# Opening loads of a GELU MLP kernel: slices of 256 KB on two queues in place of 512 KB on one

## The chip, the cores and the metric

The kernel runs on one core of a Trainium2 chip. Its engines work side by side and meet at semaphores: TensorE (PE in the profile, its weight loads PEld), VectorE (DVE), ScalarE (ACT), GpSimd (POOL) and SyncE (SP, which here only issues DMA requests). The core has 16 DMA engines; requests reach them through queues, of which SyncE, ScalarE and GpSimd each have their own. The metric is the device time of one execution in microseconds.

## The reference

```python
m, k, n, p = 1024, 1024, 2048, 1024     # a: m x k, b: k x n, c: n x p, all fp32
h = np.matmul(a, b)
h = 0.5 * h * (1 + np.tanh(np.sqrt(2 / np.pi) * (h + 0.044715 * h ** 3)))
return np.matmul(h, c).astype(np.float32)
```

Two matrix products with a GELU (tanh form) between them.

## The kernel before

All products run on 128 x 128 tiles and accumulate in PSUM, which has eight banks of 128 x 512 fp32. The first product needs a with its contraction index on the partitions, so every 128 x 128 tile of a is turned on TensorE (a transpose against an identity matrix) and copied by VectorE from PSUM into the tile aT, which is bf16. In aT the first index is the half of the rows of a (h = 0 or 1, 512 rows each) and the second is the contraction slice k, eight slices of 128. b lies in b1 (columns 0 to 1023) and b2 (columns 1024 to 2047), c in c_sb, all bf16. The result of the first product is kept, after GELU, in hT.

The first 512 columns of b are multiplied in the plain way: tile t of 128 columns, half h, accumulates over the eight slices (functions mm1 and block). The remaining columns of b, and the whole second product, go through a scheme with seven products in place of eight (class Seven); it needs sums and differences of quarters, which VectorE and ScalarE make. All of that comes after the change and is not touched by it.

The order of work on every engine is the order in which it is written; nothing is reordered. Loads come on two queues:

- SyncE's queue brings fp32 data as it is: into sta a quarter of the contraction (256 columns of a, two slices) for one half of the rows, 512 KB at a time, and into stb slices of b. In order: a(half 0, quarter 0), b slices 0 and 1, a(1,0), a(0,1), b slice 2 (lines 75 to 79). These have to be cast to bf16 by VectorE or ScalarE (cast_a, cast_b, copy; lines 108 and 110).
- GpSimd's queue casts while it loads, into abq (a) and b1 (b). It starts behind a copy of one element of sta, the "gate" of line 81, so it starts when the first load has landed. Its order: a(1,1), b slice 3, then for quarters 2 and 3 a(0,q), b(q), a(1,q), then the rest of b and all of c. At most eight of its requests are under way: the ninth waits for the landing of the first.

PE begins with "stir" products on zeros (line 125), which compute nothing that is kept. Then it turns a(0,0), multiplies slice 0 and 1 of half 0, and so on, with the turning of the next quarter always between blocks of products. Line 145 is a transpose, line 146 VectorE's copy to aT, line 114 a product of the plain part. Line 86 loads a in GpSimd's queue, lines 89, 92, 98 and 101 load b, line 104 c.

Of the kernel before, what the change touches and what calls it, by code (L numbers as in the profile page):

```python
# [9 lines left out]
F32 = mybir.dt.float32  # L10
F32R = mybir.dt.float32r
BF16 = mybir.dt.bfloat16
# [7 lines left out]
def kernel(ctx, tc, a, b, c, out):  # L20
    nc = tc.nc
    M, K = a.shape
    _, N = b.shape
    _, P = c.shape
    H = 512
# [3 lines left out]
    av = a.rearrange("(mt p) k -> p mt k", p=128)  # L29
    bv = b.rearrange("(kt p) n -> p kt n", p=128)  # L30
# [9 lines left out]
    def slot(tag, shape, dt, name):  # L40
        return big.tile(shape, dt, name=name, tag=tag)

    def bank(i, shape=(128, H), dt=F32, name="ps"):
        return pp.tile(list(shape), dt, name=name, tag=f"bank{i}", padded_shape=None)

    def pieces(tag, bufs, shape, dt, name):
        return small.tile(shape, dt, name=name, tag=tag, bufs=bufs)

    warm = nc.const_aps.tensor(0.0, [128, 256], F32)
    ident = consts.tile([128, 128], BF16, name="ident")  # L50
    make_identity(nc, ident)
    gate = consts.tile([128, 1], F32, name="gate")
# [6 lines left out]
    aT = slot("a", [128, 2, KT, H], BF16, "aT")  # L59
    b1 = slot("b1", [128, KT, 1024], BF16, "b1")  # L60
# [2 lines left out]

    KH = KT // 2
    stb = slot("x0", [128, KT, H], F32, "stb")
    sta = slot("x1", [128, 2, 2, 4, 256], F32, "sta")
    abq = slot("x3", [128, 4, 2, 4, 256], BF16, "abq")

    def a_part(h, q):
        return av[:, 4 * h:4 * h + 4, ds(q * 256, 256)]  # L70

    def b_part(q):
        return bv[:, 2 * q:2 * q + 2, 0:H]

    nc.sync.dma_start(out=sta[:, 0, 0], in_=a_part(0, 0))
    nc.sync.dma_start(out=stb[:, 0:2], in_=b_part(0))
    nc.sync.dma_start(out=sta[:, 1, 0], in_=a_part(1, 0))
    nc.sync.dma_start(out=sta[:, 0, 1], in_=a_part(0, 1))
    nc.sync.dma_start(out=stb[:, 2], in_=bv[:, 2, 0:H])

    nc.gpsimd.tensor_copy(gate, sta[:, 0, 0, 3, 0:1])  # L81
    nc.scalar.activation(g, warm[:, 0:1], AF.Gelu_apprx_tanh)


    def cast_load_a(h, q):
        nc.gpsimd.dma_start(out=abq[:, q, h], in_=a_part(h, q))  # L86

    def cast_load_b(q):
        nc.gpsimd.dma_start(out=b1[:, 2 * q:2 * q + 2, 0:H], in_=b_part(q))  # L89

    cast_load_a(1, 1)
    nc.gpsimd.dma_start(out=b1[:, 3, 0:H], in_=bv[:, 3, 0:H])  # L92
    for q in range(2, 4):
# [5 lines left out]
    for n in range(2):  # L99
        for k in range(0, KT, 4):  # L100
            nc.gpsimd.dma_start(out=b2[:, k:k + 4, ts(n, H)],
                                in_=bv[:, k:k + 4, ds(1024 + n * H, H)])
# [3 lines left out]
    def copy(eng, dst, src):  # L106
        if eng is nc.scalar:
            nc.scalar.activation(dst, src, AF.Copy)
        else:
            nc.vector.tensor_copy(dst, src)  # L110

    def mm1(p, t, h, ks):
        for k in ks:
            nc.tensor.matmul(p, b1[:, k, ts(t, 128)], aT[:, h, k],  # L114
                             start=(k == 0), stop=(k == KT - 1))
# [6 lines left out]
    def stir(*widths):  # L122

        for w in widths:
            nc.tensor.matmul(ps[0, 3][:, 0:w], warm[:, 0:128], warm[:, 0:w],
                             start=True, stop=True, skip_group_check=True)

    def cast_a(h, q, *engs):

        ab = pieces("ab", 2, [128, 4, 256], BF16, "ab")  # L130
        for i, eng in enumerate(engs):
            w = 256 // len(engs)
            for j, e in enumerate(eng if isinstance(eng, tuple) else (eng,)):
                m = slice(2 * j, 2 * j + 2) if isinstance(eng, tuple) else slice(0, 4)
                copy(e, ab[:, m, ts(i, w)], sta[:, h, q][:, m, ts(i, w)])
        return ab

    def turn(h, q, i, ab):

        banks = i if isinstance(i, tuple) else (i,)  # L140
        pts = [bank(x, (128, 2, H), BF16, "pt") for x in banks]
        for n in range(2):
            pt = pts[n % len(pts)]
            for m in range(4):
                nc.tensor.transpose(pt[:, n, ts(m, 128)], ab[:, m, ts(n, 128)], ident)  # L145
            nc.vector.tensor_copy(aT[:, h, 2 * q + n], pt[:, n])  # L146
            yield

    def cast_b(k, *engs):
        c0 = 0  # L150
        for i, eng in enumerate(engs):
            w = (H - c0) if i == len(engs) - 1 else H // len(engs) // 128 * 128
            copy(eng, b1[:, k, ds(c0, w)], stb[:, k, ds(c0, w)])
            c0 += w

    def block(h, tiles, ks):
        for k in ks:
            for t in tiles:
                mm1(ps[h, t], t, h, (k,))
# [66 lines left out]
    zero = Seven(4, quarters(b1, H, 256), BB, [None] * 4, [None] * 4, 2)  # L226
    one = Seven(4, quarters(b2, 0, H), BB, [None] * 4, zero.t)

    stir(256, 256, 256, 256, 256)
    tn = turn(0, 0, 4, cast_a(0, 0, nc.vector))  # L230
    next(tn)
    stir(128)
    cast_b(0, nc.vector, nc.vector, nc.scalar)
    next(tn)
    stir(64)
    cast_b(1, nc.scalar)
    ab = cast_a(1, 0, nc.vector, nc.scalar)
    block(0, range(4), (0,))
    block(0, range(2), (1,))
    for _ in turn(1, 0, (7, 6), ab):  # L240
        pass
    block(0, range(2, 4), (1,))
    ab = cast_a(0, 1, (nc.scalar, nc.vector), nc.vector)
    cast_b(2, nc.scalar, nc.scalar)
    for t in range(3):
        ps[1, t] = bank(4 + t)
    zero.t[0], zero.t[1] = pair(2)
    block(1, range(3), (0,))
    tn = turn(0, 1, 7, ab)
    next(tn)  # L250
    block(1, range(3), (1,))
    next(tn)
# [1 line left out]
    for q in range(1, 3):  # L254
        k = 2 * q
        block(0, range(4), (k,))
        tn = turn(1, q, 7, abq[:, q, 1])
# [5 lines left out]
        tn = turn(0, q + 1, 7, abq[:, q + 1, 0])  # L263
# [10 lines left out]
    tn = turn(1, 3, 0, abq[:, 3, 1])  # L274
# [213 lines left out]
```

## Time and profile before

| | us |
|---|---|
| median of 3 runs | 117.2 (117.19 to 117.28) |
| the profiled execution's own time | 117.6 |
| its span | 115.8 |
| PE busy | 110.7 |
| VectorE, ScalarE, GpSimd busy | 90.1, 51.4, 17.3 |
| first load of a, issue to landing | 3.7 |
| granted clock of TensorE | 1.0 of full |

The span is the stretch of the program that the profiler shows, and the execution's time includes what lies around it. A busy PE is not PE at its peak, since products overlap: the mean of 379 ns of a 128 x 512 product in bf16 is longer than the distance from one to the next. In a timeline row stand the start, the length from the first start to the last end of a merged group, the engine, the line, the operation with its tiles, the count, and in brackets the idle time before it with what ended that. A row of the windows gives for each engine the busy time and the number of its instructions, then the granted clock, the mean busy share of the DMA engines (over 1 where records overlap) and the GB/s that they wrote.

### The profile page before, as it was taken

Reading aid. Unit: us, or ns where it says so; the run is one execution under the profiler, and the core shown is the slowest. Engines: PE = TensorE matmul, PEld = TensorE weight load, DVE = VectorE, ACT = ScalarE, POOL = GpSimd, SP = SyncE. Lnnn points to the kernel's source line nnn. Section 1 sums busy time; section 2 is a strip of 40 time slices with the busy share of each in tenths; the row PEclk is TensorE's granted clock in tenths of the full one; section 3 lists DMA queues with packets and bytes.
Section 4 is the critical chain, followed back from the end, with each engine's and each line's share of the span. In section 5 each row is a group of like instructions: output and inputs, shape, how many; then the busy total and the mean of one; then the engine's idle time right before and its main releaser. Section 6 shows DMA issues by size and latency. Waiting matters only on the chain.

```text
span 115.8 us, 1473 instructions
## 1 busy us (share of the span) xinstructions
PE 110.7 (96%) x544; PEld 77.1 (67%) x550; DVE 90.1 (78%) x108; ACT 51.4 (44%) x86; POOL 17.3 (15%) x29
## 2 busy tenths in 40 slices
PE   7889999999999999999999999999999999999990
PEld 6545555445777447888886444588888888888870
DVE  0247747689999998944789999999999986964581
ACT  5053000799268998066699339700043992000000
POOL 2497754222332000000000000000000000000000
PEclk9999999999999999999999999999999999999999
DMA  3999999999999999998000000070000002004994
GB/s 74 296 381 221 200 199 204 204 207 207 205 210 210 211 212 212 212 210 163 9 0 0 6 0 0 0 272 0 0 0 0 0 0 94 2 27 173 364 358 166
DMA packets 13414, 15.94 MB, mean 138 GB/s; under 512 B 736, under 2 KB 9184, under 8 KB 13408
## 3 DMA queue, kind: packets, MB, share of 16 engines
q0 software_dynamic: 8672, 9.31, 47.6%
q1 hardware_dynamic: 4592, 6.42, 15.7%
q10 hardware_dynamic: 144, 0.13, 0.3%
q8 instruction: 4, 0.07, 0.2%
q14 instruction: 2, 0.02, 0.0%
HBM read 20.97 MB, written 4.19 MB: 217 GB/s over the span
## 4 chain that ended last, share of the span: by engine, by line
PE 79%; DMA 13%; POOL 5%; issue 0%; DVE 0%
PE ps L212 76%; DMA abq<-in_a_dram 10%; DMA sta<-in_a_dram 3%; POOL abq L86 3%; PE ps L114 2%; POOL b L89 1%; POOL gate L81 1%; PE pt L145 1%; POOL b L92 0%; DVE ot L375 0%
## 5 line engine op out<-in xcount | busy, mean ns | idle before, releaser
L212 PE MATMUL ps<-x,s 128*128 128x512 f32 x128 | 29.6, 391 | 0.0
L212 PEld LDWEIGHTS ps<-x,s 128*128 128x128 f32 x128 | 24.0, 188 | 5.1
L212 PE MATMUL ps<-x,x 128*128 128x512 f32 x96 | 22.9, 394 | 0.0
L212 PEld LDWEIGHTS ps<-x,x 128*128 128x128 f32 x96 | 18.0, 188 | 3.9
L114 PE MATMUL ps<-aT,b 128*128 128x512 bf16 x62 | 15.7, 379 | 0.3 <-DVE b L110 0.2
L298 ACT ACTIVATE v<-ps 128x512 f32<-128x512 f32 x10 | 6.0, 598 | 19.1 <-PE ps L212 19.1
L212 PE MATMUL ps<-c_sb,hT 128*128 128x512 bf16 (+2 forms) x78 | 14.1, 336 | 0.1
L212 PE MATMUL ps<-x 128*128 128x512 f32 x56 | 13.2, 393 | 0.0
L212 PEld LDWEIGHTS ps<-x 128*128 128x128 f32 x56 | 10.2, 188 | 2.7 <-ACT u L298 0.4
L212 PEld LDWEIGHTS <-hT 128*128 128x128 bf16 x80 | 7.1, 98 | 7.0 <-issue 0.5
L118 ACT ACTIVATE hT<-ps 128x512 bf16<-128x512 f32 x14 | 7.3, 596 | 9.6 <-PE ps L114 9.6
L118 ACT ACTIVATE hT<-ot 128x512 bf16<-128x512 f32 x18 | 10.4, 623 | 2.1 <-DVE ot L303 2.0
L146 DVE COPY aT<-pt 128x512 bf16<-128x512 bf16 x16 | 6.7, 422 | 5.5 <-PE pt L145 5.4
L212 PE MATMUL ps<-aT,b 128*128 128x512 bf16 x46 | 10.6, 379 | 0.1
L303 DVE TENSOR_TENSOR ot<-ps,u 128x512 f32<-128x512 f32 x10 | 6.7, 688 | 5.2 <-ACT u L298 5.2
L303 DVE TENSOR_TENSOR ot<-ps,v 128x512 f32<-128x512 f32 x10 | 6.7, 688 | 4.9 <-DMA out_dram<-ot 3.9
L170 DVE TENSOR_TENSOR x<-c_sb 128x1024 fp32r<-128x1024 bf16 x8 | 9.2, 1216 | 0.0
L114 PEld LDWEIGHTS <-b 128*128 128x128 bf16 x64 | 5.7, 97 | 4.5 <-DVE b L110 0.3
L212 PEld LDWEIGHTS <-b 128*128 128x128 bf16 x48 | 4.6, 97 | 5.7 <-issue 0.3
L104 POOL DMA_DIRECT2D c_sb<-in_c_dram x8 | 5.6, 703 | 13.4 <-DMA b<-in_b_dram 11.1
L170 DVE TENSOR_TENSOR x<-b 128x1024 fp32r<-128x1024 bf16 (+1 forms) x4 | 7.0, 1751 | 0.6 <-issue 0.6
L298 ACT ACTIVATE u<-ps 128x512 f32<-128x512 f32 x10 | 5.9, 597 | 3.4 <-PE ps L212 3.2
(44 smaller groups left out, 110.7 us busy)
## 6 DMA issues: line engine op xcount, KB each, us to landing
c_sb<-in_c_dram POOLq DMA_DIRECT2D x8, 512.0 KB, 19.7
out_dram<-ot SPq DMA_DIRECT2D x14, 256.0 KB, 2.1
b<-in_b_dram POOLq DMA_DIRECT2D x6, 512.0 KB, 15.6
sta<-in_a_dram SPq DMA_DIRECT2D x3, 512.0 KB, 6.2
abq<-in_a_dram POOLq DMA_DIRECT2D x5, 256.0 KB, 8.0
stb<-in_b_dram SPq DMA_DIRECT2D x1, 512.0 KB, 5.4
b<-in_b_dram POOLq DMA_DIRECT2D x2, 256.0 KB, 8.3
stb<-in_b_dram SPq DMA_DIRECT2D x1, 256.0 KB, 7.2
```

The source lines that it names most:

```text
L81: nc.gpsimd.tensor_copy(gate, sta[:, 0, 0, 3, 0:1])
L86: nc.gpsimd.dma_start(out=abq[:, q, h], in_=a_part(h, q))
L89: nc.gpsimd.dma_start(out=b1[:, 2 * q:2 * q + 2, 0:H], in_=b_part(q))
L104: nc.gpsimd.dma_start(out=c_sb[:, t:t + 2], in_=cv[:, t:t + 2])
L114: nc.tensor.matmul(p, b1[:, k, ts(t, 128)], aT[:, h, k], start=(k == 0), stop=(k == KT - 1))
L118: nc.scalar.activation(hT[h][:, t], p, AF.Gelu_apprx_tanh)
L145: nc.tensor.transpose(pt[:, n, ts(m, 128)], ab[:, m, ts(n, 128)], ident)
L146: nc.vector.tensor_copy(aT[:, h, 2 * q + n], pt[:, n])
L170: nc.vector.tensor_tensor(out=dst[:, r], in0=x[:, r], in1=y[:, r], op=op)
L212: nc.tensor.matmul(p[:, ds(c0, w)], l[:, k, ts(j, 128)], r[:, k, ds(c0, w)], start=(start and k == 0), stop=(k == self.kt - 1), skip_group ...
L298: nc.scalar.activation(st, p, AF.Copy)
L303: nc.vector.tensor_tensor(out=ot, in0=p, in1=st, op=ADD)
```

## The change

The loads on SyncE's queue are now slices of 128 columns of a for one half of the rows, 256 KB each: a(0) and a(1) of slice 0, then of slice 1. The two b slices are issued by ScalarE, the first at once, the second behind the activation that loads its table. a(0, quarter 1) and b slice 2 go from SyncE's queue to the head of GpSimd's, as loads that cast. Each slice of a is cast and turned by itself, half by half of its four row tiles; the casts are split between VectorE and ScalarE (those of a's first slice run on VectorE alone), and b's are all on ScalarE. The last wide stir is 128 instead of 256 columns. Half 1 of slice 0 is multiplied before half 0 of slice 1. The two slices are turned in PSUM banks 6 and 7.

```diff
-    sta = slot("x1", [128, 2, 2, 4, 256], F32, "sta")
+    sta = slot("x1", [128, 8, 4, 128], F32, "sta")
...
-    nc.sync.dma_start(out=sta[:, 0, 0], in_=a_part(0, 0))
-    nc.sync.dma_start(out=stb[:, 0:2], in_=b_part(0))
-    nc.sync.dma_start(out=sta[:, 1, 0], in_=a_part(1, 0))
-    nc.sync.dma_start(out=sta[:, 0, 1], in_=a_part(0, 1))
-    nc.sync.dma_start(out=stb[:, 2], in_=bv[:, 2, 0:H])
-
-    nc.gpsimd.tensor_copy(gate, sta[:, 0, 0, 3, 0:1])
+    def load_a(h, k):
+        nc.sync.dma_start(out=sta[:, 2 * k + h], in_=av[:, 4 * h:4 * h + 4, ts(k, 128)])
+
+    def load_b(eng, k):
+        eng.dma_start(out=stb[:, k], in_=bv[:, k, 0:H])
+
+    load_a(0, 0)
+    load_b(nc.scalar, 0)
+    load_a(1, 0)
+    load_a(0, 1)
+    load_a(1, 1)
+
+    nc.gpsimd.tensor_copy(gate, sta[:, 0, 3, 0:1])
     nc.scalar.activation(g, warm[:, 0:1], AF.Gelu_apprx_tanh)
+    load_b(nc.scalar, 1)
...
+    cast_load_a(0, 1)
+    nc.gpsimd.dma_start(out=b1[:, 2, 0:H], in_=bv[:, 2, 0:H])
     cast_load_a(1, 1)
...
+    def cast_a(h, k, *parts):
+        m0 = 0
+        for eng, m in parts:
+            r = slice(m0, m0 + m)
+            copy(eng, ab[k][:, h, r], sta[:, 2 * k + h][:, r])
+            m0 += m
+
+    def turn_one(h, k):
+        for m in range(4):
+            nc.tensor.transpose(pt[k][:, h, ts(m, 128)], ab[k][:, h, m], ident)
+
+    def keep_one(h, k):
+        nc.vector.tensor_copy(aT[:, h, k], pt[k][:, h])
...
-    stir(256, 256, 256, 256, 256)
-    tn = turn(0, 0, 4, cast_a(0, 0, nc.vector))
-    next(tn)
+    ab = [pieces("ab", 2, [128, 2, 4, 128], BF16, "ab") for k in range(2)]
+    pt = [bank(6 + k, (128, 2, H), BF16, "pt") for k in range(2)]
+    stir(256, 256, 256, 256, 128)
+    cast_a(0, 0, (nc.vector, 2), (nc.vector, 2))
+    turn_one(0, 0)
+    keep_one(0, 0)
     stir(128)
-    cast_b(0, nc.vector, nc.vector, nc.scalar)
-    next(tn)
+    cast_b(0, nc.scalar, nc.scalar)
     stir(64)
-    cast_b(1, nc.scalar)
-    ab = cast_a(1, 0, nc.vector, nc.scalar)
-    block(0, range(4), (0,))
-    block(0, range(2), (1,))
-    for _ in turn(1, 0, (7, 6), ab):
-        pass
-    block(0, range(2, 4), (1,))
-    ab = cast_a(0, 1, (nc.scalar, nc.vector), nc.vector)
-    cast_b(2, nc.scalar, nc.scalar)
+    cast_a(1, 0, (nc.vector, 2), (nc.scalar, 2))
+    cast_a(0, 1, (nc.vector, 2), (nc.scalar, 2))
+    block(0, range(2), (0,))
+    turn_one(1, 0)
+    keep_one(1, 0)
+    block(0, range(2, 4), (0,))
+    turn_one(0, 1)
+    keep_one(0, 1)
+    cast_b(1, nc.scalar, nc.scalar)
+    cast_a(1, 1, (nc.vector, 2), (nc.scalar, 2))
     for t in range(3):
         ps[1, t] = bank(4 + t)
     zero.t[0], zero.t[1] = pair(2)
     block(1, range(3), (0,))
-    tn = turn(0, 1, 7, ab)
+    block(0, range(2), (1,))
+    turn_one(1, 1)
+    keep_one(1, 1)
+    block(0, range(2, 4), (1,))
+    tn = turn(0, 1, 7, abq[:, 1, 0])
     next(tn)
```

More of the change, by code (lines that the diff above doesn't have):

```diff
@@ L126, in stir @@
                              start=True, stop=True, skip_group_check=True)
[L128 to L136, printed above, removed]
+    def cast_a(h, k, *parts):
[9 more added lines that the diff above has]
+        nc.vector.tensor_copy(aT[:, h, k], pt[k][:, h])
     def turn(h, q, i, ab):
```

## The prediction

> **What bounds the kernel now.** I read the page's engine table first, then the chain that ended last, the timeline of the first 25 us, one-microsecond windows of the DMA traffic, and the waits of each engine. Throughout, X.XX is us from the span's start, and a "row" is a line of such a view.
>
> ```profile
> span 115.8 us, 1473 instructions
> PE 110.7 (96%) x544; PEld 77.1 (67%) x550; DVE 90.1 (78%) x108; ACT 51.4 (44%) x86; POOL 17.3 (15%) x29
> ...
> 0.74 3.70 DMA sta<-in_a_dram
> ...
> 10.15 11.43 DMA abq<-in_a_dram
> 21.58 0.05 issue
> 21.63 0.40 PE pt L145 x4
> ...
> 24.87 2.81 PE ps L212 x13
> ```
>
> The span is PE: from 21.63 the chain is PE with gaps of 0.05 us. So only what happens before about 22 us can be changed by new loads, and the first question is where PE falls behind there. The chain names one DMA issued at 10.15, but the timeline says more:
>
> ```profile
> 5.14 0.88 POOL L86 DMA_DIRECT2D abq<-in_a_dram  x1
> 6.90 1.47 PE L114 MATMUL ps<-aT,b 128*128 128x512 bf16 x6 [0.17 <-DVE b L110]
> 10.03 0.39 PE L145 MATMUL pt<-ident,ab 128*128 128x128 bf16 x4
> 11.63 1.48 POOL L98 DMA_DIRECT2D b<-in_b_dram  x2 [0.66 <-DMA abq<-in_a_dram]
> 13.68 0.74 POOL L101 DMA_DIRECT2D b<-in_b_dram  x1 [0.56 <-DMA abq<-in_a_dram]
> 14.99 0.74 POOL L101 DMA_DIRECT2D b<-in_b_dram  x1 [0.57 <-DMA b<-in_b_dram]
> 15.99 0.24 PEld L145 LDWEIGHTS <-abq 128*128 128x128 bf16 x4 [0.30 <-DMA abq<-in_a_dram]
> 16.02 0.39 PE L145 MATMUL pt<-ident,abq 128*128 128x128 bf16 x4
> 16.23 0.74 POOL L101 DMA_DIRECT2D b<-in_b_dram  x1 [0.50 <-DMA abq<-in_a_dram]
> 17.56 0.74 POOL L101 DMA_DIRECT2D b<-in_b_dram  x1 [0.59 <-DMA abq<-in_a_dram]
> 21.62 0.23 PEld L145 LDWEIGHTS <-abq 128*128 128x128 bf16 x4 [0.64 <-DMA abq<-in_a_dram]
> ```
>
> First real product: 6.90. From 10.03 the groups "four transposes and three or four products" follow each other every 0.9 to 1.1 us, which is their own work. PE is then gated by work and by loads almost equally: at 15.99 the weight load waits for a(half 1, quarter 2), which landed at 15.95 by its last semaphore record. The POOL rows give the rate of its queue: each request waits for the landing of the one eight places ahead, and 512 KB of fp32 land every 1.31, 1.24 and 1.33 us, mean 1.29 us (400 GB/s read).
>
> ```profile
> 3.00:4.00 1.00, 1.00 (x4) 0.78 (x3) 0.00 (x0) 0.00 (x0) 0.00 (x0) 1.00 1.07 351
> 4.00:5.00 1.00, 0.79 (x4) 0.35 (x2) 0.54 (x1) 0.00 (x0) 0.51 (x1) 1.00 0.97 262
> 5.00:6.00 1.00, 0.67 (x6) 0.50 (x7) 0.51 (x2) 0.00 (x0) 1.00 (x2) 1.00 0.94 276
> 7.00:8.00 1.00, 1.00 (x6) 0.48 (x5) 0.32 (x2) 0.56 (x3) 1.00 (x3) 1.00 1.10 387
> 14.00:15.00 1.00, 1.00 (x10) 0.57 (x9) 0.89 (x2) 0.00 (x0) 0.43 (x2) 1.00 1.44 197
> ```
>
> Last two columns: DMA share and GB/s written. All 16 engines are full from 2 us on (in the last row 197 GB/s written is twice that read, because POOL's queue casts). While the first b load runs (4 to 6) the rate falls to 262 and 276; with 1 KB rows of a it is 387. In the packet records POOL's first packet starts only at 8.82, 3.68 us after its issue, and each engine takes it up as that engine's SyncE packets end (8.89 to 9.76, mean 9.21): POOL's loads wait until SyncE's are through. I call 9.21 the hand-over.
>
> **The change, part by part.**
>
> *The DMA sum.* Up to a(1,2) the same 4.5 MB come in both kernels; 0.75 MB (a(0,1) and slice 2 of b) move from SyncE's queue to the head of POOL's. Before, a(1,2) landed 15.95 - 9.21 = 6.74 us after the hand-over; with 0.75 MB more, at 1.29 per 0.5 MB, that is 6.74 + 1.94 = 8.68. So the change is neutral if its hand-over is at 9.21 - 1.94 = 7.27. When is it? Model: first packet at 2.0; a with its packet time; b with its own. Check on before: 1.5 MB of a at 46 ns per 1 KB packet on 16 engines (356 GB/s) 4.42; the first 512 KB of b at about 270 (windows 4 to 6) 1.94; the last 256 KB at 84 ns per 2 KB (390) 0.67; sum with 2.0: 9.03, so 0.2 of start-up is missing. After: 1 MB of a now in rows of 512 B. No load of before has those; the final 64 KB stores do, at 27 ns (303 GB/s), hence 3.46; the ends are 3.46 and 2.7 (the 387 of window 7). The 512 KB of b: 1.94 as in windows 4 to 6, or 1.34 at 84 ns. I take the row nearest to each: the same 512 KB of b as the slow ones, the same 512 B packet. 2.0 + 0.2 + 3.46 + 1.94 = 7.6 (bounds 6.24 and 7.6). a(1,2) then lands at 7.6 + 8.68 = 16.28, 0.33 later than 15.95; PE had 0.07 to spare (16.02), so it is late by 0.26.
>
> *POOL.* The gate copy waits for the first a load, now 256 KB beside 256 KB of b: the same bytes as before, 4.3 against 4.44; gate 0.70, issue at 5.0 instead of 5.14. Two more issues (0.88, 0.55 as L86 and L92 now) stand before the rest; at 0.75 each against 1.29 of transfer they cost nothing while eight are in flight. The ninth request is now b's last pair and waits for a(0,1), the tenth is a(1,3): issued at about 10.5, needed in the queue at 17, hidden by 6 us. What is open is how soon after 5.0 POOL's first packet can run: at most 3.68 us (8.68, 1.4 late against 7.27), at least its 0.88 of issue (5.9, hidden behind 7.6). I take hidden, since before the engines themselves were the visible cause. The Trainium skill (DMA: Bandwidth & Descriptors, "Latency and other measured facts") gives about 1 us for the first byte from POOL; the hand-over would then hide it, and no run here shows it alone. The same page ("Queues, rings and completion order") says that an engine alternates between queue rows packet by packet; by that, POOL's loads would share from about 6.4, the last 0.4 MB of SyncE's would take twice as long and PE's start would be 0.8 late. The row differs: no POOL packet ran before an engine was through with SyncE's, and the row decides.
>
> *SyncE and ScalarE queues.* SyncE issues four instead of five, 0.42 to 0.51 each, from 0.74 to 2.7, each under 0.85 us of transfer: covered. ScalarE issues b0 at 0.74 and b1 behind table load (1.28) and activation (0.20), at about 2.7: 0.5 each in front of casts that start after 4; covered by the wait of 4.4 for stb. b1's first packet comes at 2.7 + 1.25 = 3.95, while a's are running: no hole.
>
> *PE, VectorE, ScalarE up to the group that stood at 10.03.* Landing of a00 4.3; two 128x256 casts of 0.28 (before one of 0.69); four transposes to 5.35 (0.40); copy 0.42, so 5.8. The stirs of 128 and 64 behind it (0.44, 0.39) hold PE to 6.2; one 256 stir less 0.4 ahead is idle time. b0's two ScalarE casts (0.42 each) end before 5.5. From 6.2: eleven products at 0.215 to 0.23 and three transposes at 0.25 to 0.40: 3.1 to 3.7, so 9.3 to 9.9, if casts keep up. VectorE has the cast of a01 queued ahead of the copy of a10's transpose; a01 lands around 6.7, copy to 7.6, and its first user (half 1, slice 0) stands at 7.5 to 8. ScalarE casts a10, a01, b1 (twice), a11 in that order, 0.42 each: the last lands about 8.2, so 8.65, transposes 9.05, copy 9.5, and the next group uses the same bank, about 9.6 to 9.9. This is before 10.03, so PE's earlier start (6.2 against 6.90) is worth up to 0.4 and is then given back at the wait for a(1,2).
>
> *Behind 16.* PE is filled by its own work until a(1,3), which landed at 21.58 although 15 of its 16 engines were through by 19.92: a 16 KB instruction fetch started at 19.57 on the last one. The fetch goes by PE's place in the program, so it moves with PE: 0. Later loads shift by the same 0.3; nothing past 30 us waits for one.
>
> Sum: +0.26 on the profiled execution, whose own time is 117.6 with a span of 115.8 and 1.8 around it; it stands 0.4 above the median of the three runs, 117.2. Forecast 117.2 + 0.26 = 117.5. No change is within 0.2%, 0.23 us, about what a measurement can tell.
>
> **The rivals.**
> 1. *Hand-over early, gain.* If 512 B rows and the two hardware queues together run at the 387 of window 7, and b at 390, the hand-over comes at 6.24; POOL's first packet, if it takes 1.9 (its bounds are 0.88 and 3.68), at 6.9. Then a(1,2) lands at 15.6, 0.37 early, and PE's 9.6 allows it: 116.8. A gain is decided by a hand-over before 7.0. For it: b's slow windows may have been a first touch that now overlaps a's packets. Against it: 27 ns per 512 B.
> 2. *Break-even.* Half of b slow: 2.0 + 0.2 + 3.46 + 1.64 = 7.3; PE unchanged, 117.2.
> 3. *POOL's first packet late.* 3.68 after 5.0: hand-over 8.68, a hole in DMA traffic from about 7.5; 1.4 late less 0.07: 118.5. For it: the 3.68 is the only latency shown. Against: it coincides engine by engine with the end of SyncE's packets.
> 4. *b behind a.* If ScalarE's queue waits behind SyncE's as POOL's did, b0 lands at about 6.5 and ScalarE's seven casts (2.9) end at 9.4, transposes and copy 10.3: PE 0.3 late, 117.5, the same as the forecast by another road.
>
> **How the numbers follow.** Forecast 0.30, rival 4 0.07, rival 3 0.10 (slower: 0.47), rival 2 0.24, rival 1 0.29. The range has rival 1's 0.6 gain with half of a further early hand-over below (116.6) and rival 3 above (118.5); beyond are about 1 in 10 below and 1 in 12 above. The forecast's own range is 117.4 to 117.9.
>
> **What would show it.** Right: 512 B packets near 27 ns; POOL's first packet near 7.6; the first product near 6.2; a weight load waiting for abq near 16.3; nothing new after 22. Wrong: POOL's first packet before 7.0 with PE ahead (rival 1), a fall of DMA share to near 0 about 7 to 8 (rival 3), ScalarE's b casts first at 6.5 (rival 4), or a stall of PE on VectorE's a01 cast.

## The result and the profile after

The changed kernel takes 121.25 us (121.12 to 121.37) beside 117.21 us of the kernel before on the same chip: a ratio of 1.0343, 95% interval 1.0325 to 1.0361. That is 4.0 us slower. The forecast was 117.5 us with a range up to 118.5: the sign was right, the size was not. The profiled execution took 121.37 us with a span of 119.6; against the profiled execution of before (117.6, span 115.8) both are 3.8 us longer.

From the page, the span, the engine table and the shares of the chain:

```profile
span 119.6 us, 1481 instructions
PE 112.6 (94%) x550; PEld 78.1 (65%) x550; DVE 89.5 (75%) x107; ACT 51.2 (43%) x87; POOL 18.1 (15%) x31
...
PE 84%; DMA 10%; POOL 2%; DVE 0%; issue 0%
```

The chain that ended last, cut to where it changes hands:

```profile
0.74 5.53 DMA sta<-in_a_dram
...
8.71 7.02 DMA b<-in_b_dram
...
15.78 1.04 PE ps L123 x4
...
19.73 0.40 PE pt L159 x4
...
28.27 88.03 PE ps L226 x408
```

The work of PE from the first product of the seven-product scheme on is as long as it was; it starts at 28.27 where it had started at 24.87, 3.4 us later. (The other 0.4 us of the span lie behind VectorE's last sum.) So the loss is all made before 28 us, and two loads carry it: the first one, of 256 KB, needs 5.53 us where 512 KB had needed 3.70, and slice 3 of b, the fourth request of GpSimd's queue, needs 7.02 us from its issue, most of it behind slice 2. The timeline shows what each does to PE:

```profile
6.02 0.72 ACT L117 ACTIVATE b<-stb 128x256 bf16<-128x256 f32 x2 [3.32 <-DMA stb<-in_b_dram]
6.30 0.49 DVE L119 CAST ab<-sta 128x256 bf16<-128x256 f32 x2 [6.30 <-DMA sta<-in_a_dram]
6.57 0.87 POOL L93 DMA_DIRECT2D abq<-in_a_dram  x1
6.65 0.61 PE L147 MATMUL pt<-ident,ab 128*128 128x128 bf16 x4 [1.69 <-POOL gate L87]
7.44 0.55 POOL L99 DMA_DIRECT2D b<-in_b_dram  x1
7.90 1.06 PE L123 MATMUL ps<-aT,b 128*128 128x512 bf16 x2
12.13 0.38 PE L159 MATMUL pt<-ident,abq 128*128 128x128 bf16 x4
15.78 1.04 PE L123 MATMUL ps<-aT,b 128*128 128x512 bf16 x4 [0.81 <-DMA b<-in_b_dram]
19.73 0.23 PEld L159 LDWEIGHTS <-abq 128*128 128x128 bf16 x4 [0.49 <-DMA abq<-in_a_dram]
```

The casts of a start at 6.30 (before: first a landed at 4.44), GpSimd's first request goes out at 6.57 (5.14), PE stands idle for 1.69 us and makes its first product at 7.90 (6.90), and that pair of products takes 1.06 us where six had taken 1.47: the second starts 0.43 after the first, twice the distance of 0.22 that the same products have at full clock. The clock record of after begins at 9.76, so the clock column of the windows says nothing of this moment; the distance does. The four transposes of a(0, quarter 1) follow at 12.13, where those of before stood at 10.03. Then PE waits for b at 15.78 and for a(1, quarter 2) at 19.73; the same wait stood at 15.99 before. The DMA windows show the two holes (the last two columns are the share of the DMA engines and the GB/s written):

```profile
2.00:3.00 1.00, 1.00 (x3) 0.78 (x3) 0.00 (x0) 0.69 (x2) 0.00 (x0) 1.00 0.61 162
3.00:4.00 1.00, 1.00 (x4) 0.77 (x3) 0.00 (x0) 0.00 (x0) 0.00 (x0) 1.00 0.90 144
...
10.00:11.00 1.00, 1.00 (x9) 0.52 (x7) 0.62 (x2) 0.00 (x0) 1.00 (x3) 1.00 1.15 102
11.00:12.00 1.00, 1.00 (x8) 0.51 (x7) 0.35 (x1) 0.00 (x0) 1.00 (x2) 1.00 0.77 43
12.00:13.00 1.00, 0.92 (x8) 0.51 (x7) 0.50 (x2) 0.00 (x0) 0.92 (x2) 1.00 1.02 125
13.00:14.00 1.00, 1.00 (x9) 0.51 (x7) 0.55 (x2) 0.00 (x0) 0.70 (x1) 1.00 1.42 197
```

From 3 to 4 us 144 GB/s arrive (before 351) although the engines are 0.90 busy: the packets themselves are slow. From 10 to 13 the queue of GpSimd writes 102, 43 and 125 where 197 is its normal rate. The packet records name the packets: in the first hole the 2 KB packets of slice 0 of b, at a median of 164 to 277 ns in the half microseconds from 3.0 to 4.5 and up to 651 (84 ns later); in the second hole the 1 KB packets of slice 2 of b in GpSimd's queue, up to 1333 ns (98 ns later).

The same records put the hand-over (the mean end of SyncE's packets) at 8.05. The prediction's own rule, a(1,2) lands 8.68 us after the hand-over, gives 16.73; it landed at 19.69. Hence the arithmetic that the runs below have to explain: 0.78 us from a hand-over later than the neutral 7.27, and 2.96 us behind the hand-over, where the second hole lies, together the 3.74 by which a(1,2) is late. The rule sets a mean over the 16 engines (the hand-over) against the last of them (the landing). In the changed kernel the last engine is 0.83 behind the mean when a(1,2) lands (18.86 and 19.69), in the kernel before 0.38 (15.57 and 15.95). By the means, 2.5 us are left for the hole, and 0.45 is that the engines end further apart. (In the six kernels below that have no second hole, what the rule leaves by the means is under 0.2.)

### The profile page after: what moved, and what is told of

The parts are those of the page before. It is cut to its first block, busy times and chain, and to the rows that moved or that the text cites. A ratio compares the mean times of both kernels' runs of the same rounds, so it can differ in the third digit from the quotient of the medians.

```text
span 119.6 us, 1481 instructions
## 1 busy us (share of the span) xinstructions
PE 112.6 (94%) x550; PEld 78.1 (65%) x550; DVE 89.5 (75%) x107; ACT 51.2 (43%) x87; POOL 18.1 (15%) x31
## 4 chain that ended last, share of the span: by engine, by line
PE 84%; DMA 10%; POOL 2%; DVE 0%; issue 0%
PE ps L226 74%; PE ps L123 8%; DMA b<-in_b_dram 6%; DMA sta<-in_a_dram 5%; PE pt L159 2%; POOL abq L93 1%; POOL b L99 0%; POOL gate L87 0%; DVE ot L396 0%
## 5 line engine op out<-in xcount | busy, mean ns | idle before, releaser
L123 PE MATMUL ps<-aT,b 128*128 128x512 bf16 x64 | 17.2, 392 | 0.8 <-DMA b<-in_b_dram 0.8
L226 PE MATMUL ps<-aT,b 128*128 128x512 bf16 x48 | 10.7, 379 | 0.0
L160 DVE COPY aT<-pt 128x512 bf16<-128x512 bf16 x12 | 5.1, 424 | 6.3 <-PE pt L159 6.3
```

Source lines behind the costliest of these rows:

```text
L123: nc.tensor.matmul(p, b1[:, k, ts(t, 128)], aT[:, h, k], start=(k == 0), stop=(k == KT - 1))
L226: nc.tensor.matmul(p[:, ds(c0, w)], l[:, k, ts(j, 128)], r[:, k, ds(c0, w)], start=(start and k == 0), stop=(k == self.kt - 1), skip_group ...
```

## The experiments

Four causes are on trial. *Late queue*: GpSimd's queue has the second hole because it is started late. *Two queues*: b on ScalarE's queue holds up the first load of a. *Slices*: a in rows of 512 B makes the fp32 loads longer in itself. *Clock*: PE's idle time costs it its clock. The rival to *two queues*, for the first hole, is that b's reads are slow by themselves, whoever issues them. Times are medians, ratios go against the kernel before on the same chip (117.2 to 117.4); positions within a kernel come from its profiled execution.

| kernel | us | ratio, 95% interval | first a landed | SyncE's end, mean | first b of GpSimd's queue: issue, first packet | a(1,2) landed | PE takes it up |
|---|---|---|---|---|---|---|---|
| before | 117.2 | 1 | 4.44 | 9.21 | 6.01, 10.35 | 15.95 | 16.02 |
| after | 121.25 | 1.034 (1.033 to 1.036) | 6.28 | 8.05 | 7.44, 9.81 | 19.69 | 19.73 |
| move alone | 119.24 | 1.017 (1.013 to 1.020) | 4.30 | 6.79 | 5.87, 8.35 | 17.56 | 17.61 |
| move, early queue | 117.49 | 1.001 (0.998 to 1.004) | 4.17 | 7.17 | 3.87, 8.00 | 16.19 | 16.24 |
| b on ScalarE alone | 119.93 | 1.025 (1.020 to 1.029) | 6.35 | 9.09 | 7.92, 10.31 | 17.22 | 18.54 |
| after, early queue | 120.20 | 1.023 (1.017 to 1.029) | 6.19 | 8.06 | 5.62, 8.98 | 17.11 | 18.83 |
| after, b pair in GpSimd's queue | 120.61 | 1.027 (1.020 to 1.033) | 6.18 | 7.94 | 7.36, 9.63 | 18.47 | 18.77 |
| after, more stirs | 120.65 | 1.029 (1.021 to 1.037) | 6.20 | 8.06 | 7.37, 9.52 | 18.93 | 18.98 |
| after, early queue and stirs | 119.11 | 1.014 (1.008 to 1.021) | 6.33 | 7.98 | 5.61, 8.92 | 17.32 | 17.39 |
| after, all on SyncE | 118.65 | 1.012 (1.009 to 1.015) | 3.35 | 8.08 | 4.52, 8.77 | 16.77 | 16.81 |
| the same, b as one pair behind one a | 118.88 | 1.013 (1.009 to 1.017) | 3.39 | 8.10 | 4.56, 9.08 | 17.23 | 17.27 |
| the same, b pair behind two a | 120.30 | 1.025 (1.022 to 1.029) | 3.39 | 8.03 | 4.56, 8.77 | 17.25 | 19.10 |

The last two columns say what holds PE at a(1, quarter 2): where they are within 0.1 us, PE waits for the load; where they are further apart, PE comes late by itself.

### The move to GpSimd's queue alone

The kernel before, with only a(0, quarter 1) and slice 2 of b moved to the head of GpSimd's queue; everything else, the 512 KB loads too, stays.

```diff
-    nc.sync.dma_start(out=sta[:, 0, 1], in_=a_part(0, 1))
-    nc.sync.dma_start(out=stb[:, 2], in_=bv[:, 2, 0:H])
...
+    cast_load_a(0, 1)
+    nc.gpsimd.dma_start(out=b1[:, 2, 0:H], in_=bv[:, 2, 0:H])
     cast_load_a(1, 1)
...
-    ab = cast_a(0, 1, (nc.scalar, nc.vector), nc.vector)
-    cast_b(2, nc.scalar, nc.scalar)
...
-    tn = turn(0, 1, 7, ab)
+    tn = turn(0, 1, 7, abq[:, 1, 0])
```

> The kernel before with one part of the change alone: a(0,1) and slice 2 of b move from SyncE's queue to the head of GpSimd's. The three 512 KB loads stay as they are. Theory A (moving 0.75 MB to GpSimd's queue costs nothing as long as that queue is ready when SyncE's ends): hand-over at about 7.3, no slow window, time 117.0 to 117.6. Theory B (a single slice of b at the head of GpSimd's queue is read slowly there): the window around b slice 2 falls below 130 GB/s written and the time is 119 or more.

Measured: 119.24 us (118.79 to 119.58). The hand-over came at 6.79, half a microsecond before the neutral 7.27, so by the prediction's rule this kernel should have gained; a(1,2) would have landed at 15.47. It landed at 17.56, because the hole is there in full. The windows of this kernel:

```profile
8.00:9.00 1.00, 0.92 (x11) 0.66 (x11) 0.51 (x3) 0.31 (x1) 1.00 (x2) 1.00 1.26 154
9.00:10.00 1.00, 0.94 (x6) 0.25 (x4) 0.36 (x2) 0.00 (x0) 1.00 (x3) 1.00 0.59 38
10.00:11.00 1.00, 1.00 (x10) 0.62 (x11) 0.42 (x1) 0.00 (x0) 1.00 (x2) 1.00 0.58 51
```

So the second hole needs neither the slices of 256 KB nor ScalarE's queue: the move alone brings it, and costs 2.0 us.

### The same move with an early queue

Here GpSimd does not wait for the first load of a; a fill of two tiles of c_sb, which the loads of c overwrite later, takes the place of the gate copy.

```diff
-    nc.gpsimd.tensor_copy(gate, sta[:, 0, 0, 3, 0:1])
+    nc.gpsimd.memset(c_sb[:, 12:14], 0.0)
```

> The kernel before with a(0, quarter 1) and slice 2 of b moved to the head of GpSimd's queue, as in the run that made this move alone, but GpSimd's first request does not wait for the first load of a: the gate copy is replaced by a fill of two tiles of c_sb (one such fill took 1.8 us), so the first request goes out near 3 instead of 5.0. Theory that a late start of that queue makes its first b request slow: no stretch under 150 GB/s written between 8 and 12, SyncE's packets still end near 6.8, a(1,2) lands near 15.5 (6.8 + 8.68), PE goes at its own pace: 116.6 to 117.3. Rival, that slice 2 of b is slow in that queue whenever it comes first: a stretch of 40 to 60 GB/s again within 7 to 11, a(1,2) near 17.5, 118.8 to 119.6 as with the late start. A middle case, that the early requests take bytes from the first fp32 loads: first a load after 4.8, SyncE's end after 7.3, 117.3 to 118.2.

Measured: 117.49 us beside 117.27, ratio 1.0007 (0.9979 to 1.0035): no difference from before. GpSimd's first request and the same windows:

```profile
3.00 0.87 POOL L84 DMA_DIRECT2D abq<-in_a_dram  x1
```

```profile
8.00:9.00 1.00, 1.00 (x11) 0.51 (x10) 0.43 (x1) 0.63 (x1) 0.82 (x1) 1.00 1.38 202
9.00:10.00 1.00, 1.00 (x9) 0.50 (x7) 0.76 (x2) 0.00 (x0) 0.31 (x1) 1.00 1.39 194
10.00:11.00 1.00, 1.00 (x9) 0.53 (x8) 0.42 (x1) 0.00 (x0) 1.00 (x2) 1.00 1.36 199
```

The hole is gone, and nothing but the start of GpSimd's queue was changed (3.00 in place of 5.00). The same slice of b, in the same place of the same queue, is read at full rate when its request has waited 4.1 us before its first packet, and slowly when it has waited 2.5. That settles, for this queue behind SyncE's loads, the theory of the late queue against its rival; how the late start makes the reads slow is not shown. The middle case has a small part in it: SyncE's end moved from 6.79 to 7.17 and a(1,2) came at 16.19, not 15.5, and PE took it up 0.22 later than in the kernel before, as much as the time is above 117.27. The time is 0.2 above the interval named, and not a gain.

### The changed kernel with an early queue

```diff
-    nc.gpsimd.tensor_copy(gate, sta[:, 0, 3, 0:1])
+    for t in (12, 14):
+        nc.gpsimd.memset(c_sb[:, t:t + 2], 0.0)
```

> The changed kernel with GpSimd's queue no longer behind the first load of a: two fills of a part of c_sb that is loaded later stand in place of the gate copy, so that its first request goes out at about 4 to 5 instead of 6.57. Theory D (the 16 engines run dry at the hand-over and then start GpSimd's queue together, and b's slice 2 is read slowly because of that): no slow stretch from 10 to 13, a(1,2) lands at about 17, time 118 to 118.8. Theory B: the stretch stays and the time is above 120.5. Had GpSimd's packets to share with the hardware queues, the last fp32 load would land after 10 instead of 9.20.

Measured: 120.20 us (119.00 to 120.46), 1.05 less than the changed kernel. The second hole is gone here too: 219, 192, 186 and 198 GB/s written in the windows from 8 to 12. The time is above the 118 to 118.8 that theory D named, because PE does not use the loads:

```profile
7.00:8.00 1.00, 0.85 (x7) 0.71 (x8) 0.62 (x3) 0.34 (x1) 1.00 (x2) 0.99 1.19 329
8.00:9.00 1.00, 1.00 (x6) 0.48 (x5) 0.90 (x2) 0.67 (x3) 1.00 (x3) 0.50 1.43 219
9.00:10.00 1.00, 1.00 (x6) 0.44 (x4) 0.43 (x2) 0.74 (x3) 1.00 (x2) 0.50 1.31 192
10.00:11.00 1.00, 1.00 (x7) 0.63 (x6) 0.43 (x2) 0.00 (x0) 0.69 (x2) 0.50 1.36 186
```

The third number from the end is the granted clock: 0.50 from 7.97 to 11.39 by the clock record, after a stretch of full clock from 4.56 to 7.97 in which PE had stood idle for 1.74 us. PE comes to the transposes of a(0, quarter 1) at 12.84 and is bound by its own work behind that; it takes up a(1, quarter 2) 1.7 us after its landing at 17.11:

```profile
12.84 0.38 PE L160 MATMUL pt<-ident,abq 128*128 128x128 bf16 x4
18.83 0.39 PE L160 MATMUL pt<-ident,abq 128*128 128x128 bf16 x4
```

Two stretches of 3.41 us: the Trainium skill (TensorE: Matmul & The Clock Gate, "What's actually happening") gives windows of about 3.4 us at whose end the clock is set by how busy PE was, and this record agrees.

This run also shows when GpSimd's packets run: its first request went out at 4.74, its first packet came at 7.64 on engines that SyncE's packets had left, and the last fp32 load was not delayed (9.11 against 9.20).

### Slices 2 and 3 of b as one request in GpSimd's queue

```diff
-    nc.gpsimd.dma_start(out=b1[:, 2, 0:H], in_=bv[:, 2, 0:H])
+    cast_load_b(1)
     cast_load_a(1, 1)
-    nc.gpsimd.dma_start(out=b1[:, 3, 0:H], in_=bv[:, 3, 0:H])
```

> The changed kernel with slices 2 and 3 of b in one 512 KB request of GpSimd's queue, between a(0,1) and a(1,1), as the later quarters have it. If the slow stretch from 10 to 13 belongs to requests of a single slice, it is gone: a(1,2) lands at about 17, time near 120.2 (as with the early queue, where the stretch was gone too). If it belongs to b being read by engines that start together, it stays, and may be longer: 121 or more.

Measured: 120.61 us (120.39 to 120.81), 0.6 less than the changed kernel. The hole is milder (93 GB/s written in its lowest window, where the changed kernel falls to 43), a(1,2) lands at 18.47, and PE runs at half clock from 8.35 to 11.77. So fewer and larger requests don't remove the hole. That they soften it is not shown: the kernel with more stirs below has the requests of the changed kernel, and its hole is milder too (59 GB/s written, a(1,2) at 18.93). The time fell between the two that the expectation named, and this run does not choose between causes.

### b on ScalarE's queue alone

The kernel before, with its 512 KB pair of b issued by ScalarE at 0.74.

```diff
-    nc.sync.dma_start(out=stb[:, 0:2], in_=b_part(0))
+    nc.scalar.dma_start(out=stb[:, 0:2], in_=b_part(0))
```

> The kernel before with the 512 KB load of b slices 0 and 1 issued by ScalarE instead of SyncE, nothing else. Theory C (two hardware queues that start together delay the first load of a, because b's slow packets take turns with it): the first load of a lands at 5.5 to 6.5 instead of 4.44, GpSimd's queue is issued that much later, time 117.8 to 119. Rival (queues share, bytes are bytes): the first load of a lands under 5.2 and the time is within 0.4 of 117.2.

Measured: 119.93 us (119.75 to 120.65), 2.7 slower than before, with one word changed. The timeline:

```profile
6.37 0.69 DVE L110 CAST ab<-sta 128x1024 bf16<-128x1024 f32 x1 [6.37 <-DMA sta<-in_a_dram]
7.12 0.61 PE L145 MATMUL pt<-ident,ab 128*128 128x128 bf16 x4 [1.74 <-POOL gate L81]
9.05 2.12 PE L114 MATMUL ps<-aT,b 128*128 128x512 bf16 x6
```

The first load of a lands at 6.35 in place of 4.44. The packet records say how: from 3.0 to 5.0, SyncE's queue moves 57, 47, 33 and 56 packets per half microsecond, and ScalarE's 57, 46, 32 and 53. The engines take as many packets of one queue as of the other, so each 1 KB packet of a (46 ns) has a 2 KB packet of b beside it, and those are the ones that take long. The Trainium skill (DMA: Bandwidth & Descriptors, "Queues, rings and completion order") has that alternation; between these two queues the run agrees, while GpSimd's packets, as the early queue showed, wait until an engine has nothing of SyncE's; there the measurement differs from the page, and it decides. PE stands at half clock until its clock record begins at 10.37 (its products are 0.43 apart at 9.05), and is bound by its own work afterwards: a(1,2) landed at 17.22 and was taken up at 18.54.

The second hole is here as well (169, 56 and 74 GB/s written from 10 to 13), on slice 3 of b, the first b request of GpSimd's queue in this kernel, which waited 2.4 us. So it does not hang on slice 2, and with SyncE's packets running until 9.09 it is not that the engines had run dry before it.

### All fp32 loads of the changed kernel in SyncE's queue

```diff
-    load_b(nc.scalar, 0)
+    load_b(nc.sync, 0)
     load_a(1, 0)
     load_a(0, 1)
+    load_b(nc.sync, 1)
     load_a(1, 1)
...
-    load_b(nc.scalar, 1)
```

> The changed kernel with all six fp32 loads in SyncE's queue, in the order a0 of slice 0, b slice 0, a1 of slice 0, a0 of slice 1, b slice 1, a1 of slice 1. Theory C: the first a lands at about 3.5 instead of 6.28, GpSimd issues at about 4.2 and is ready long before SyncE's queue ends; if the slow stretch from 10 to 13 comes from GpSimd's queue starting late, it goes too, and the time is 117 to 118. Theory B (slice 2 of b is slow in GpSimd's queue by itself): the stretch stays and the time is 119.5 to 120.5.

Measured: 118.65 us (118.43 to 118.89): 2.6 of the 4.0 us are back, though the time stays above the 117 to 118 of theory C. Windows and timeline of this kernel:

```profile
3.00:4.00 1.00, 1.00 (x4) 0.77 (x3) 0.49 (x2) 0.00 (x0) 0.59 (x2) 1.00 0.96 137
4.00:5.00 1.00, 1.00 (x10) 0.90 (x8) 0.00 (x0) 0.00 (x0) 1.00 (x2) 1.00 0.57 113
```

```profile
3.65 0.87 POOL L93 DMA_DIRECT2D abq<-in_a_dram  x1
6.38 0.61 PE L123 MATMUL ps<-aT,b 128*128 128x512 bf16 x2 [0.94 <-ACT b L117]
16.81 0.23 PEld L159 LDWEIGHTS <-abq 128*128 128x128 bf16 x4 [0.54 <-DMA abq<-in_a_dram]
```

The first a lands at 3.35, so the gate opens at 3.65 by itself, no second hole follows, and PE's first product (6.38) is earlier than that of before. One step undoes the first a's delay, the clock gap and the late queue at once. What is left: the hand-over is at 8.08 as in the changed kernel, 0.81 behind the neutral 7.27, and a(1,2) lands at 16.77, 0.82 behind 15.95. Here the rule of the prediction (8.08 + 8.68 = 16.76) is exact. The first hole is still there, with slice 0 of b in the same queue as a (packets up to 1036 ns): the slow first reads of b don't come from the second hardware queue. That queue only decides whether a has to wait for them.

### b as one pair in SyncE's queue, at two places

Both kernels have b's two slices as one request of 512 KB in SyncE's queue, the first behind one slice of a, the second behind two.

```diff
     load_a(0, 0)
-    load_b(nc.scalar, 0)
+    nc.sync.dma_start(out=stb[:, 0:2], in_=b_part(0))
     load_a(1, 0)
...
-    load_b(nc.scalar, 1)
```

> The changed kernel with its fp32 loads in SyncE's queue alone and b slices 0 and 1 in one 512 KB request, as before: a0 of slice 0, the b pair, a1 of slice 0, a0 and a1 of slice 1. Slicing a, the move to GpSimd's queue and the order of casts and products stay. Theory H (the loss comes from b: two queues at once and single slices of b; the slicing of a costs little): first a at 3.35, b pair at about 5.7, SyncE's packets end at 7.3 to 7.6, a(1,2) at 16.1 to 16.4, time 117.2 to 118.0, which is what the prediction's sum describes. Rival (the 512 B rows of a, or b slice 2 in GpSimd's queue, cost the rest): 118.5 or more.

> As the other of this pair, with both halves of a's slice 0 ahead of the b pair. Theory H with b slow only where it runs behind a single request of a: b's packets stay at 84 ns longer, SyncE's packets end at 7.2 or earlier, time 117.0 to 117.8; PE starts a little later (b lands at about 6.2). If b's first read is slow wherever it stands, the end of SyncE's packets is the same as in the other and the time equal or up to 0.4 longer.

Measured: 118.88 us (118.26 to 119.95) and 120.30 us (119.75 to 121.37), both above what theory H named. Their SyncE's packets end at 8.10 and 8.03, not at the 7.3 to 7.6 that a cost of splitting b would have left. So the split of b is not what makes the hand-over late. In all eight kernels here with a in 512 B rows SyncE's end lies between 7.94 and 8.10, whichever queue b is in and however it is cut; the two kernels that load the same 1.5 MB with a in 1 KB rows end at 6.79 and 7.17. 1 MB of a costs 2048 x 27 ns / 16 = 3.46 us in 512 B packets and 1024 x 46 / 16 = 2.94 in 1 KB packets, so by this estimate 0.5 of the 0.9 to 1.3 us is the price of shorter rows. The rest was not separated.

The second of the two also shows the clock again. Its pair of b landed at 7.75:

```profile
8.24 1.04 PE L122 MATMUL ps<-aT,b 128*128 128x512 bf16 x2 [2.70 <-ACT b L116]
```

PE, idle for 2.70 us, then works at half clock from 8.07 to 11.48 and comes to a(0, quarter 1) at 13.11 (11.18 in the first, which kept its clock in the profiled execution). The executions of the first price the clock directly: three were granted a mean of 0.997 to 1.0 and took 118.3 to 118.4 us, three 0.983 to 0.986 and took 119.3 to 120.0, 1.2 us more in the median. At full clock, then, the first is no slower than the kernel with six single requests in SyncE's queue (118.4 to 118.9).

### More stirs, alone and with the early queue

Four more wide products on zeros bridge PE's wait for the first a.

```diff
-    stir(256, 256, 256, 256, 128)
+    stir(256, 256, 256, 256, 256, 256, 256, 256, 128)
```

> The changed kernel with four more stirs of 256 columns at its start, so that PE does not stand idle from 4.96 to 6.65. Theory W (PE's clock fell to half in that gap, which alone costs nothing, since PE waits for loads at 15.78 and 19.73): first products 0.22 instead of 0.43 apart, time 120.8 to 121.4 as before. Rival (the slow clock is on the path): 119.5 or less.

> Both: GpSimd's queue early, as in the run before, and four more stirs. With the slow stretch of the loads gone, PE's slow clock was what held the early kernel at 120.2: its chain from 8.6 to 12.8 should shrink by 1.5 to 2 us. Theory W: 118.2 to 118.8, with PE waiting for a(1,2) at about 17.0. If the clock had no part in it: 120 again.

Measured: 120.65 us (120.55 to 121.32), 0.6 less than the changed kernel; and together with the early queue 119.11 us (118.88 to 119.45), 2.1 less, and 1.1 less than the early queue alone. The first pair of products now takes its usual time, and PE waits for a(1, quarter 2) in both kernels (below, the first two rows are of the stirs alone, the third of both):

```profile
7.58 0.59 PE L123 MATMUL ps<-aT,b 128*128 128x512 bf16 x2
18.97 0.23 PEld L159 LDWEIGHTS <-abq 128*128 128x128 bf16 x4 [0.53 <-DMA abq<-in_a_dram]
17.36 0.23 PEld L160 LDWEIGHTS <-abq 128*128 128x128 bf16 x4 [0.31 <-DMA abq<-in_a_dram]
```

Without the second hole the clock is worth 1.1 us: the early queue alone leaves PE behind its loads, and with the stirs it waits for them again. With the hole nothing is shown to hang on the clock. The changed kernel also waits for a(1,2), and the stirs' 0.6 us go with a landing 0.76 earlier (18.93 against 19.69), although stirs touch no load; the intervals of the two ratios overlap (1.021 to 1.037 and 1.033 to 1.036). That is theory W, with a time a little under the 120.8 that it named. With both causes gone the kernel is still 1.4% slower than before: PE waits for a(1,2) at 17.36, with the hand-over at 7.98 and the first a at 6.33.

### Reads by themselves

Two kernels that only read asked whether b's slow packets are a matter of the first touch or of what runs beside them.

```diff
+    read_a(0, one_a[0])
+    read_a(1, one_a[0])
+    for k in range(8):
+        read_b(nc.sync, k, one_b[0])
...
```

> Leaves out all of the computation: it only reads and writes back something. In SyncE's queue, 256 KB each and each waiting until the one before has landed: two slices of a, the eight slices of b (512 columns), the same eight again, four slices of a; then eight slices of b (the next 512 columns) back to back; then four pairs of b slices, one after the other; then in GpSimd's queue four slices of b one after the other and four back to back. Theory L (16 engines that start a slice of b at the same moment get in each other's way): every b slice that waits for the one before is slow, the second time as well, 2 us of packets or more, packets near 250 ns; the slices of a are not; back to back only the first is slow. Theory F (the first touch of b is slow): only the first slice of b, or each slice the first time, is slow; the second pass runs at 84 ns a packet, 256 KB in about 0.7 us of packets.

```diff
+    apart()
+    first()
+    load(second, bv[:, 0, 0:H])
+    apart()
...
```

> Leaves out all of the computation: nine trials of two requests in SyncE's queue, the second right behind the first, with everything landed in between. Trials: 1 and 2, a slice of a (256 KB, rows of 512 B) and then slice 0 of b (rows of 2 KB, 8 KB apart); 3, a slice of a and another; 4, a and a pair of b slices (512 KB); 5, a and the same slice of b as two requests of 256 columns; 6, slice 1 of b and then slice 0; 7, a and slice 5 of b at other columns; 8, a and 128 rows of c (2 KB each, 4 KB apart); 9, a and slice 2 of b with rows of 4 KB. The packet records time the second request from its first packet to its last. Theory G (a slice of b is read slowly whenever all 16 engines come to it together out of an earlier request; in the trial before, alone, it took 1.75 us with 84 ns packets): 2.5 us or more in trials 1, 2, 7, packets of 200 to 1000 ns, trial 3 near 1 us, trials 4, 8 and 9 less slow per byte if other row distances matter. Theory F (first touch): trial 1 slow, trial 2 not.

Here first() loads 256 KB of a, the load behind it 256 KB of b, and apart() makes the next group wait until all has landed; the groups that follow change the second load.

Measured in the first: slices of b one at a time take 3.0 us from issue to landing with packets of 84 ns, in the first pass as in the second (3.01 and 3.03). A first touch alone costs nothing. Only the very first slice, issued right behind a load of a, was slow: 3.91 us, with packets up to 1365 ns. A row of slices of b behind slices of a, in columns not read before, was slow again at the change from a to b (up to 1431 ns), and fast from then on. On GpSimd's queue with nothing else running, the first packet came 1.23 to 1.37 us after the issue. Four slices of b that had not been read before came one by one through that queue with packets of 101 to 104 ns in the mean, 98 being usual. So a short wait does not make b slow by itself: in the kernels it did so where GpSimd's packets took over from SyncE's.

Measured in the second, the landing of the second load behind that of the first: slice 0 of b the first time 2.21 us, the same slice again 1.09, a 1.20, another slice of b not read before 1.18, a pair of b (512 KB) 1.56, slice 0 as two requests 1.79, slice 0 behind slice 1 of b 1.22, slice 2 in rows of 4 KB (512 KB) 2.09, rows of c 0.69. Theory G wanted 2.5 us or more from first to last packet for slice 0, its repeat and the new slice; they took 2.49, 1.62 and 1.48. The windows of this kernel (of engines it lists VectorE and GpSimd alone) show the first two, the slow one from 4 and the quick one from 10 us:

```profile
5.00:6.00 1.00, 0.00 (x0) 0.00 (x0) 1.00 0.45 90
6.00:7.00 1.00, 0.00 (x0) 0.00 (x0) 1.00 0.14 47
...
10.00:11.00 1.00, 0.00 (x0) 0.00 (x0) 1.00 0.99 304
11.00:12.00 1.00, 0.00 (x0) 0.00 (x0) 1.00 0.53 178
```

So neither "first touch" (another new slice was quick) nor "behind a" (the repeat was quick) explains the slow reads in its plain form. What is shown: the first reads of b in a program are slower than later ones in these two kernels and in all twelve of the table. In the twelve, the first 128 packets take 115 to 221 ns in the mean where 84 is usual: 115 to 136 in five of the six kernels that load b in a pair (177 in the sixth, behind two slices of a), 190 in one queue as a slice of its own, and 204 to 221 as a slice of its own on ScalarE's queue, the changed kernel's form. Why, stays open; so does why GpSimd's first b request is slow in these kernels when it waited 2.1 to 2.5 us and not when it waited 3.3 or more.

## Why the prediction was wrong, point by point

- **What bounds the kernel, and where.** Right: nothing new is lost after 22 us (PE takes up a(1,2) 3.71 later than before and the first product of the scheme only 3.40 later), the 16 KB instruction fetch moved with PE (from 19.57 to 23.48), and the wait for a(1,2) is where PE's lead or lag is decided.
- **The model of the hand-over, 7.6.** It was 8.05. The packet time of 27 ns for 512 B was right. The bound was not one: 7.6 was called the upper end, because the slow windows of b (270 GB/s) were taken as the slowest that b could be. In the changed kernel 144 GB/s stood in such a window. Of a(1,2)'s 3.74 us this term makes 0.78 where 0.33 had been given. In the kernel with all fp32 loads on one queue, which has neither the second hole nor the clock gap, PE takes up a(1,2) 0.79 late, the profiled execution is 0.8 longer than that of before, and the median 1.4.
- **POOL's queue at 1.29 us per 512 KB, from its first packet on. This is the step that failed most.** The rate was read off rows between 13.7 and 17.6, where the queue had long been running, and set for its whole length, its first microseconds included. It fell to 43 GB/s written, and this costs 2.5 to 3.0 of the 3.74 us (an early queue alone brings a(1,2) from 19.69 to 17.11). In the kernel before the first b request of the queue waited 4.34 us for its first packet; in the changed one 2.37. Starting the queue early removes the hole in both pairs of runs; what makes the reads slow behind a late start stays open. The prediction had "issue at 5.0" and a hand-over at 7.6, so by its own numbers it saw the lead shrink from 3.68 to 2.6, and costed that at nothing as long as the packets came in time.
- **"The same bytes as before, 4.3" for the first load of a.** It landed at 6.28. Two loads on two hardware queues don't share bytes, their packets ran in equal numbers, and b's were the ones that took long. The prediction weighed alternation only between POOL and SyncE, where it does not happen, and not between SyncE and ScalarE, where it does. Gate, GpSimd's issue (5.0, was 6.57), first product (6.2, was 7.90) and the group of a(0, quarter 1) (9.6 to 9.9, was 12.13) all follow. The late issue is not needed for the second hole (the move alone, issued at 5.00 as predicted, has it), but it does not leave the queue the lead that would avoid it.
- **"One 256 stir less 0.4 ahead is idle time", at nothing.** Its cover was a first a at 4.3. PE then idled 1.69 us, and the full clock came at 9.76 where before it had come at 4.04. In the changed kernel the loads hide this; with the second hole gone it is worth 1.1 us.
- **Rivals.** Rival 3 had the right kind of event, a hole in the DMA traffic that sets a(1,2), but not its cause: POOL's first packet came 1.58 after its issue, not 3.68. Rival 4 is turned round: a waited for b. Rival 1 falls by the 512 B rows (8.05). The early hand-over that it needed did come in the move alone (6.79), and gave a gain neither there nor with an early queue.
- **What a(0,1) and slice 2 of b cost in GpSimd's queue.** "Neutral" was right as the sum had it: with an early queue the move is 117.49 against 117.27.

The 4.0 us do not split into a sum, since the causes overlap: the early queue alone gives back 1.05, the stirs alone 0.6 (not clear of noise), both 2.1; one hardware queue, which removes the wait of a, the clock gap and the late queue together, gives back 2.6. The last 1.4 stays with the kernel that loads a in slices: 0.8 of it is the later landing, and the rest was not separated. No version here is faster than the kernel before.

## What to carry to other kernels

A second hardware queue did not add bandwidth at the start of this kernel (SyncE's packets ended at 9.09 with b on ScalarE's queue, at 9.21 without): its packets ran one for one with the first queue's, and as they were larger and slower, the load that everything waits for suffered. A rate taken from the middle of a queue says nothing of its first request; look at how long before its data that request was issued, and try an earlier start (here a fill in place of a gate) before moving work into it. When a first load may come late, give PE something to do until then, and read the distance between two products beside the clock column. Before a gain is put down to the clock, look whether PE waits for a load behind it.

## What the runs showed of the hardware

- SyncE's and ScalarE's queues send equal numbers of packets while both have work (57 and 57, 47 and 46, 33 and 32, 56 and 53 packets in successive half microseconds), while GpSimd's packets began on an engine only after SyncE's (issued 4.74, first packet 7.64).
- The first 128 packets of b, rows of 2 KB, took 115 to 221 ns in the mean and single ones up to 1480 ns in the twelve kernels; the same read a few microseconds later had a median of 84.
- The first b request of GpSimd's queue came with a microsecond of 38 to 93 GB/s written where it had waited 2.1 to 2.5 us for its first packet (five kernels), and with none that low where it had waited 3.3 us or more (seven kernels; lowest seen 165). In a kernel that only reads, a wait of 1.23 to 1.37 us in an otherwise idle queue left the packets at 101 to 104 ns in the mean.
- Full clock is granted and taken away in stretches of 3.41 us (4.56 to 7.97, 7.97 to 11.39); idle times of 1.60 to 2.70 us went with half clock in the stretch that followed (1.60, 1.74 and 2.70 in three kernels), and 1.56 in another kernel did not.
